# The 16 zb projection tiles: each 512-token matmul issued as two of 256 tokens, into two banks

## The chip, the cores and the metric

The kernel runs on one core of one Trainium2 chip. The time is device microseconds of one execution of the whole program. The kernel before took 2508.1 us (median of 3 runs, 2506.12 to 2508.59).

## The reference

One layer of a hybrid encoder trunk over 512 tokens of width 2048, all in float32. After an RMS norm `h` is multiplied by one wide weight matrix; its columns feed two branches, and one slice of it, `z_b` (2048 columns), is the gate of the convolution branch:

```python
h = rmsnorm(x, g_pre[i])
proj = h @ w_in[i]
qkv, z_a, b_raw, a_raw, glu_in, z_b, gate_logits = jnp.split(proj, ...)
...                                   # branch A: gated DeltaNet -> y_a
u = jax.nn.glu(glu_in, axis=-1)
u = causal_depthwise_conv(u, w_dw[i]) + b_dw[i]
u = jax.nn.silu(layernorm(u, ln_g[i], ln_b[i])) * jax.nn.silu(z_b)
y_b = u @ w_br_b[i]
gate_a, gate_b = jnp.split(jax.nn.sigmoid(gate_logits + b_gate[i]), 2, axis=-1)
mixed = (gate_a * y_a + gate_b * y_b) @ w_out[i]
x = x + rmsnorm(mixed, g_post[i])
...                                   # per-layer embedding -> output
```

## The kernel before

A projection is computed channel-major: one tile is 128 output channels (partitions of a PSUM bank) by all 512 tokens. Its inner dimension is 2048, in 16 slabs of 128. To keep float32 precision with the one-pass type fp32r, each operand is split into a high and a low part, and three products are summed: high weight by high `h`, high weight by low `h`, low weight by high `h` (lines 182, 184, 186 of `gemm_cm`). A tile is thus 16 x 3 = 48 matmuls, each with a 128x128 weight block as the stationary operand and 128x512 of `hT` as the moving one, all 48 summed into one bank. A weight block is loaded anew for each matmul: the page counts as many weight loads as matmuls (12202 each).

The weights arrive by DMA in pieces of 128x1024; `prep` cuts each in two, ScalarE rounds the high half (`CAST`, L127) and VectorE subtracts to get the low half (L128). The ring of split pieces holds four; one piece feeds 12 matmuls.

The order is written out by hand. Tiles are jobs in a list; after every matmul `tick()` is called, and it advances generators such as `layer_norm` every so many ticks, so their instructions fall between the matmuls. The 16 zb tiles (`evac_zb`, L828: SiLU from PSUM by ScalarE) stand after the tiles of branch A and before the gate-b and w_br_b tiles; while they run, `layer_norm` runs beside them: it sums means on TensorE (`mean_ps`, L779, and `rstd_ps`, L806, two passes of 128x512 fp32 each; `var_ps`, L794, four products of one column), works on VectorE, ScalarE and GpSimd, and at its end multiplies by each `zb[i]` (L817).

In this stretch two PSUM pools are open: `gps` (2 banks, tiles `g`) and `lps` (2 banks, the norm's). Two other loops are spoken of below: `gemm_tm` (L1212 to L1214), which walks over four banks and does three matmuls in each before it goes to the next, and the head scan's small fp32 products (`psB`, L468, 128x128).

Of the kernel before, what the change touches and what calls it, by code (L numbers as in the profile page):

```python
# [9 lines left out]
F32 = mybir.dt.float32  # L10
F32R = mybir.dt.float32r
AF = mybir.ActivationFunctionType
# [3 lines left out]
P = 128  # L16
T = 512
NTT = T // P
D = 2048
NK = D // P  # L20
# [12 lines left out]
ZB_TILE0 = 97  # L33
# [49 lines left out]
def _body(ctx, tc, A, out):  # L83
    nc = tc.nc
    PSUM = bass.MemoryType.PSUM
    mm = nc.tensor.matmul
# [27 lines left out]
    prep_src = deque()  # L114
    prepped = deque()

    def prep():
        if not prep_src:
            return
        src = prep_src.popleft()  # L120
        raw = rawp.tile([P, 1024], F32, tag="raw", name="raw", bufs=3)
        nc.sync.dma_start(raw, src)
        for q in range(2):
            rq = raw[:, q * T:(q + 1) * T]
            w = ring.tile([P, 1024], F32R, tag="w", name="w")
            hi, lo = w[:, 0:T], w[:, T:]
            nc.scalar.copy(hi, rq)  # L127
            nc.vector.tensor_tensor(lo, rq, hi.bitcast(F32), ALU.subtract)  # L128
            prepped.append((hi, lo))

    def next_piece():
        while len(prepped) < 3 and prep_src:
            prep()
        return prepped.popleft()

    jobs = deque()
# [5 lines left out]
    def tick():  # L142
        for a in list(active):
            a[2] -= 1
            if a[2] <= 0:
                steps = next(a[0], "end")
                if steps == "end":
                    active.remove(a)
                else:
                    a[2] = steps or a[1]  # L150
# [7 lines left out]
    def run_jobs():  # L158
        while jobs:
            jobs.popleft()()  # L160
# [3 lines left out]
    gps = gps_ctx.enter_context(tc.tile_pool(name="gps", bufs=2, space=PSUM))  # L164

    def w_in_tile(t):
        return A["w_in"][t]

    def gemm_cm(src, rhs, evac):
        if src is not None:  # L170
            prep_src.extend([src[0], src[1]])

        def job():
            ps = gps.tile([P, T], F32, tag="g", name="g")
            for qt in range(4):
                hi, lo = next_piece()
                for kk in range(4):
                    k = qt * 4 + kk
                    rh, rl = rhs[k]
                    wh = hi[:, kk * P:(kk + 1) * P]  # L180
                    wl = lo[:, kk * P:(kk + 1) * P]
                    mm(ps, wh, rh, start=(k == 0), stop=False)  # L182
                    tick()
                    mm(ps, wh, rl, start=False, stop=False)  # L184
                    tick()
                    mm(ps, wl, rh, start=False, stop=(k == NK - 1))  # L186
                    tick()
            evac(ps)
        jobs.append(job)

    hT = []
# [544 lines left out]
    def low(n, name, dt=F32R):  # L736
        return lop.tile([P, T], dt, tag="lop", name=name) if n < LOP else s2.tile([P, T], dt, tag="s2", name=name)
# [87 lines left out]
    def evac_zb(i):  # L825
        def f(ps):
            z = low(0, "zb", F32)
            nc.scalar.activation(z, ps, AF.Silu)  # L828
            zb[i] = z
        return f  # L830

    jobs.append(lambda: spawn(layer_norm(), 10))
    for i in range(NK):
        gemm_cm(w_in_tile(ZB_TILE0 + i), hT, evac_zb(i))
    mixT = [None] * NK

    def evac_yb(i):
# [79 lines left out]
        gemm_cm(A["w_br_b"][i], uT, evac_yb(i))  # L917
    lnp_ctx = ExitStack()
    lnp = lnp_ctx.enter_context(tc.tile_pool(name="lnp", bufs=1))
    lps = lnp_ctx.enter_context(tc.tile_pool(name="lps", bufs=2, space=PSUM))  # L920
    run_jobs()
    lnp_ctx.close()
# [140 lines left out]
    def run(products, side=None):  # L1063
        ps = {}
        for q in range(4):
            for pr in products:
                piece = next_piece_sw()
                if q == 0:
                    ps[pr] = [bank() for _ in range(2)]
                for t in range(2):  # L1070
                    mms(ps[pr][t], pr, piece, q, t)
                if side:
                    side()
        return ps
# [68 lines left out]
    def stepper(gen, n=1):  # L1143
        def f(k=None):
            for _ in range(n):
                next(gen, None)
        return f
# [9 lines left out]
    ps = run(("P1", "Q5"), stepper(gen))  # L1157
# [6 lines left out]
    ps = run(("P6", "P7", "P3"), stepper(gen))  # L1164
# [7 lines left out]
    ps = run(("P2", "Q4"))  # L1172
# [5 lines left out]
    ps = run(("P1", "Q5"))  # L1178
# [5 lines left out]
    ps = run(("P6", "P3"))  # L1184
# [4 lines left out]
    ps = run(("P2",))  # L1189
# [3 lines left out]
    ps = run(("P7",), stepper(pgen))  # L1193
# [5 lines left out]
    ps = run(("Q4",), stepper(pgen, 3))  # L1199
# [84 lines left out]
    for tt in range(NTT):  # L1284
        ps = fps.tile([P, T], F32, tag="f", name="f")
        for k in range(NK):
            wh, wl = held[k]
# [71 lines left out]
```

## Time and profile before

| | |
|---|---|
| median of 3 runs | 2508.1 us (2506.12 to 2508.59) |
| the profiled execution | 2505.59 us, span 2503.8 us |
| TensorE matmul busy | 2472.1 us, 99% of the span, 12202 matmuls |
| TensorE weight load busy | 2037.6 us, 81%, 12202 loads |
| VectorE / ScalarE busy | 1655.5 us (66%) / 1053.2 us (42%) |
| granted TensorE clock | 0.999 of full over the span |

How to read it: matmuls are pipelined, so a row's duration (395 ns for 128x512) is longer than the distance from one start to the next. What a matmul costs the engine is that distance, and it is read from starts in the order of time. PE is the matmul, PEld the weight load, which is shown beside it. Times in rows are in us from the span's start, durations of one instruction in ns where a column says mean.

### The profile page before, as it was taken

Reading aid. Unit: us, or ns where it says so; the run is one execution under the profiler, and the core shown is the slowest. Engines: PE = TensorE matmul, PEld = TensorE weight load, DVE = VectorE, ACT = ScalarE, POOL = GpSimd, SP = SyncE. Lnnn points to the kernel's source line nnn. Section 1 sums busy time; section 2 is a strip of 40 time slices with the busy share of each in tenths; the row PEclk is TensorE's granted clock in tenths of the full one; section 3 lists DMA queues with packets and bytes.
Section 4 is the critical chain, followed back from the end, with each engine's and each line's share of the span. In section 5 each row is a group of like instructions: output and inputs, shape, how many; then the busy total and the mean of one; then the engine's idle time right before and its main releaser. Section 6 shows DMA issues by size and latency. Waiting matters only on the chain.

```text
span 2503.8 us, 32581 instructions
## 1 busy us (share of the span) xinstructions
PE 2472.1 (99%) x12202; PEld 2037.6 (81%) x12202; DVE 1655.5 (66%) x3092; ACT 1053.2 (42%) x2083; POOL 133.6 (5%) x151
## 2 busy tenths in 40 slices
PE   8999999999999999999999999999999999998998
PEld 7888888888888888888888888888888888786886
DVE  6776767767677766886877879947323334877644
ACT  6555555555645555322222222235322223544532
POOL 0100000100000000000000000011000000100000
PEclk9999999999999999999999999999999999999999
DMA  7322222222122222323232323422222222776542
GB/s 260 118 94 71 93 72 85 81 81 91 66 92 81 77 85 76 110 97 109 97 109 97 107 99 110 169 85 102 99 100 94 97 97 100 189 229 196 202 169 76
DMA packets 85406, 279.45 MB, mean 112 GB/s; under 512 B 9472, under 2 KB 9728, under 8 KB 85248
## 3 DMA queue, kind: packets, MB, share of 16 engines
q1 hardware_dynamic: 81792, 266.89, 30.8%
q0 software_dynamic: 2304, 8.39, 1.8%
q10 hardware_dynamic: 1152, 2.10, 0.3%
q8 instruction: 95, 1.56, 0.2%
q14 instruction: 63, 0.52, 0.1%
HBM read 262.66 MB, written 14.68 MB: 111 GB/s over the span
## 4 chain that ended last, share of the span: by engine, by line
PE 93%; DVE 3%; DMA 2%; issue 1%; ACT 0%; POOL 0%; SPq 0%; DVEq 0%; POOLq 0%; ACTq 0%
PE g L184 26%; PE g L186 25%; PE g L182 25%; PE f L1213 2%; PE f L1214 2%; PE f L1212 2%; DMA raw<-in_w_out 2%; PE psB L468 1%; PE psS L474 1%; PE psA L462 1%; PE f L1057 1%; PE f L1058 1%; PE f L1056 1%; DVE wsp L1033 1%; PE pg L569 1%
## 5 line engine op out<-in xcount | busy, mean ns | idle before, releaser
L186 PE MATMUL g<-hh,w 128*128 128x512 f32 x2320 | 915.8, 395 | 1.6 <-DVE w L128 1.6
L184 PE MATMUL g<-hl,w 128*128 128x512 f32 x2320 | 916.3, 395 | 0.0
L182 PE MATMUL g<-hh,w 128*128 128x512 f32 x2320 | 913.5, 394 | 0.0
L128 DVE TENSOR_TENSOR w<-raw,w 128x512 fp32r<-128x512 f32 x780 | 552.8, 713 | 446.5 <-ACT w L127 444.5
L127 ACT CAST w<-raw 128x512 fp32r<-128x512 f32 x780 | 478.0, 618 | 879.1 <-PE g L186 777.6
L186 PEld LDWEIGHTS g<-hh,w 128*128 128x128 f32 x2320 | 436.5, 188 | 88.9 <-DVE w L128 4.7
L184 PEld LDWEIGHTS g<-hl,w 128*128 128x128 f32 x2320 | 436.4, 188 | 86.3 <-issue 1.6
L182 PEld LDWEIGHTS g<-hh,w 128*128 128x128 f32 x2320 | 436.5, 188 | 84.2 <-issue 0.2
L689 DVE SCALAR_TENSOR_TENSOR uc<-sg,vec,uc 128x511 f32<-128x511 f32 (+14 forms) x480 | 351.6, 734 | 14.0 <-ACT uc L686 3.9
L410 DVE SCALAR_TENSOR_TENSOR cv<-g,vec,cv 128x511 f32<-128x511 f32 x144 | 106.4, 739 | 31.1 <-ACT cv L408 30.8
L186 PE MATMUL g<-oh,w 128*128 128x512 f32 x256 | 99.7, 389 | 0.0
L182 PE MATMUL g<-uh,w 128*128 128x512 f32 x256 | 99.7, 389 | 0.0
L182 PE MATMUL g<-oh,w 128*128 128x512 f32 x256 | 99.7, 389 | 0.0
L184 PE MATMUL g<-ul,w 128*128 128x512 f32 x256 | 99.7, 389 | 0.0
L186 PE MATMUL g<-uh,w 128*128 128x512 f32 x256 | 99.7, 389 | 0.0
L184 PE MATMUL g<-ol,w 128*128 128x512 f32 x256 | 99.7, 389 | 0.0
L604 DVE TENSOR_TENSOR prod<-UT,VT 128x2 f32<-128x2 f32 (+30 forms) x248 | 87.4, 353 | 6.6
L1057 PE MATMUL f<-wsp,oph 128*128 128x512 f32 x192 | 76.3, 398 | 5.9 <-DVE wsp L1033 5.9
L1056 PE MATMUL f<-wsp,oph 128*128 128x512 f32 x192 | 74.7, 397 | 2.8 <-ACT wsp L1032 2.7
L1213 PE MATMUL f<-w,xh 128*128 128x512 f32 x192 | 75.1, 391 | 2.0 <-DVE w L128 2.0
L1058 PE MATMUL f<-wsp,opl 128*128 128x512 f32 x192 | 75.2, 393 | 0.0
L1212 PE MATMUL f<-w,xh 128*128 128x512 f32 x192 | 75.2, 392 | 0.0
(298 smaller groups left out, 2661.3 us busy)
## 6 DMA issues: line engine op xcount, KB each, us to landing
raw<-in_w_in SPq DMA_DIRECT2D x290, 512.0 KB, 3.2
raw<-in_w_ple_gate SPq DMA_DIRECT2D x40, 512.0 KB, 3.9
raw<-in_w_out SPq DMA_DIRECT2D x35, 512.0 KB, 4.9
raw<-in_w_br_a SPq DMA_DIRECT2D x32, 512.0 KB, 3.3
raw<-in_w_br_b SPq DMA_DIRECT2D x32, 512.0 KB, 3.2
t<-in_w_out POOLq DMA_DIRECT2D x16, 512.0 KB, 8.1
rw<-in_w_out SPq DMA_DIRECT2D x9, 512.0 KB, 4.6
x<-in_x SPq DMA_DIRECT2D x8, 512.0 KB, 9.4
```

The lines of the kernel that those rows point to most:

```text
L127: nc.scalar.copy(hi, rq)
L128: nc.vector.tensor_tensor(lo, rq, hi.bitcast(F32), ALU.subtract)
L182: mm(ps, wh, rh, start=(k == 0), stop=False)
L184: mm(ps, wh, rl, start=False, stop=False)
L186: mm(ps, wl, rh, start=False, stop=(k == NK - 1))
L410: nc.vector.scalar_tensor_tensor(y[:, s:], ps[:, 0:T - s], vv(w0 + 3 - s), y[:, s:], ALU.mult, ALU.add)
L689: nc.vector.scalar_tensor_tensor(y[:, s:], u[:, 0:T - s], vv(w0 + TAPS - 1 - s), y[:, s:], ALU.mult, ALU.add)
L1056: mm(ps, lh, wh[:, c], start=kk == 0, stop=False)
L1057: mm(ps, lh, wl[:, c], start=False, stop=False)
L1058: mm(ps, ll, wh[:, c], start=False, stop=kk == 7)
L1212: mm(ps[tt], lh, wh, start=k == 0, stop=False)
L1213: mm(ps[tt], lh, wl, start=False, stop=False)
```

## The change

`gemm_halves` replaces `gemm_cm` for the 16 zb tiles alone. For each of the 48 products it issues two matmuls with the same weight block: tokens 0 to 255 into the first half of a `gps` bank, tokens 256 to 511 into the first half of a bank of a new pool `nps` (2 banks). `tick()` is called after each pair, so a tile still has 48 ticks. The SiLU is done in two halves, one from each bank.

```diff
+    def gemm_halves(src, rhs, evac):
+        prep_src.extend([src[0], src[1]])
+
+        def job():
+            ps = [gps.tile([P, T], F32, tag="g", name="g"), nps.tile([P, T], F32, tag="n", name="n")]
+            for qt in range(4):
+                hi, lo = next_piece()
+                for kk in range(4):
+                    k = qt * 4 + kk
+                    rh, rl = rhs[k]
+                    wh = hi[:, kk * P:(kk + 1) * P]
+                    wl = lo[:, kk * P:(kk + 1) * P]
+                    for m, (w, r) in enumerate(((wh, rh), (wh, rl), (wl, rh))):
+                        for n in range(2):
+                            mm(ps[n][:, 0:256], w, r[:, n * 256:n * 256 + 256],
+                               start=k == 0 and m == 0, stop=k == NK - 1 and m == 2)
+                        tick()
+            evac(ps)
+        jobs.append(job)
...
             z = low(0, "zb", F32)
-            nc.scalar.activation(z, ps, AF.Silu)
+            for n in range(2):
+                nc.scalar.activation(z[:, n * 256:n * 256 + 256], ps[n][:, 0:256], AF.Silu)
             zb[i] = z
...
     for i in range(NK):
-        gemm_cm(w_in_tile(ZB_TILE0 + i), hT, evac_zb(i))
+        gemm_halves(w_in_tile(ZB_TILE0 + i), hT, evac_zb(i))
...
     lnp = lnp_ctx.enter_context(tc.tile_pool(name="lnp", bufs=1))
+    nps = lnp_ctx.enter_context(tc.tile_pool(name="nps", bufs=2, space=PSUM))
     lps = lnp_ctx.enter_context(tc.tile_pool(name="lps", bufs=2, space=PSUM))
```

On TensorE, at the first zb tile (the two rows ahead are the end of a w_br_a tile; `hh` and `hl` are high and low `hT`, `w` the split weights, `g` and `n` the banks), there stood before:

```order
6780 L184 MATMUL g<-ol,w 128x512
6781 L186 MATMUL g<-oh,w 128x512
6782 L182 MATMUL g<-hh,w 128x512
6783 L184 MATMUL g<-hl,w 128x512
6784 L186 MATMUL g<-hh,w 128x512
6785 L182 MATMUL g<-hh,w 128x512
```

and there stands now:

```order
6780 L184 MATMUL g<-ol,w 128x512
6781 L186 MATMUL g<-oh,w 128x512
6782 L205 MATMUL g<-hh,w 128x256
6783 L205 MATMUL n<-hh,w 128x256
6784 L205 MATMUL g<-hl,w 128x256
6785 L205 MATMUL n<-hl,w 128x256
6786 L205 MATMUL g<-hh,w 128x256
6787 L205 MATMUL n<-hh,w 128x256
```

Each row of 512 tokens has become two rows of 256 on alternating banks; the products stand in the same order, and the norm's own matmuls stand between the same products as before.

On ScalarE, at the sixth zb tile, where the norm's squares (`lsq`) share the engine with the weight casts and the SiLU, there stood before:

```order
803 L127 CAST w<-raw 128x512
804 L828 ACTIVATE zb<-g 128x512
805 L127 CAST w<-raw 128x512
806 L787 ACTIVATE lsq<-ur 128x512 x4
807 L127 CAST w<-raw 128x512
```

and there stands now:

```order
808 L127 CAST w<-raw 128x512
809 L849 ACTIVATE zb<-g 128x256
810 L849 ACTIVATE zb<-n 128x256
811 L127 CAST w<-raw 128x512
812 L807 ACTIVATE lsq<-ur 128x512 x4
813 L127 CAST w<-raw 128x512
```

The SiLU is two rows, at the same place between the casts; nothing else has moved here.

## Rows read from the trace of the kernel before

**Rows 1.** The page: span, busiest engine, the chain that ended last.
```profile
span 2503.8 us, 32581 instructions
...
PE 2472.1 (99%) x12202; PEld 2037.6 (81%) x12202; DVE 1655.5 (66%) x3092; ACT 1053.2 (42%) x2083; POOL 133.6 (5%) x151
...
PE 93%; DVE 3%; DMA 2%; issue 1%; ACT 0%; POOL 0%; SPq 0%; DVEq 0%; POOLq 0%; ACTq 0%
```

**Rows 2.** Busy time by engine over the zb tiles; last: clock, DMA share, GB/s.
```profile
1613.70:1793.20 179.50, 177.93 (x784) 146.15 (x783) 99.31 (x145) 76.79 (x130) 22.52 (x14) 1.00 0.31 109
```

**Rows 3.** Order of time, TensorE matmuls, in a zb tile: start, duration, instruction.
```profile
1639.90 0.39 PE L182 MATMUL g<-hh,w 128*128 128x512 f32 x1
1640.12 0.39 PE L184 MATMUL g<-hl,w 128*128 128x512 f32 x1
1640.35 0.39 PE L186 MATMUL g<-hh,w 128*128 128x512 f32 x1
```

**Rows 4.** The same stretch, weight loads.
```profile
1639.90 0.19 PEld L184 LDWEIGHTS g<-hl,w 128*128 128x128 f32 x1
1640.13 0.19 PEld L186 LDWEIGHTS g<-hh,w 128*128 128x128 f32 x1
```

**Rows 5.** Order of time, ScalarE, over one zb tile.
```profile
1624.46 0.60 ACT L828 ACTIVATE zb<-g 128x512 f32<-128x512 f32 x1 [0.80 <-PE g L186]
1624.95 0.61 ACT L127 CAST w<-raw 128x512 fp32r<-128x512 f32 x1
1627.18 0.62 ACT L127 CAST w<-raw 128x512 fp32r<-128x512 f32 x1 [1.61 <-PE g L186]
...
1635.34 0.60 ACT L828 ACTIVATE zb<-g 128x512 f32<-128x512 f32 x1 [2.10 <-PE g L186]
```

**Rows 6.** Order of time around the norm's mean (two fp32 passes of 512 columns), and the weight load behind.
```profile
1672.31 1.02 PE L779 MATMUL mean_ps<-acc,cst 128*128 128x512 f32 x2
1672.74 0.19 PEld L186 LDWEIGHTS g<-hh,w 128*128 128x128 f32 x1 [0.24 <-issue]
```

**Rows 7.** Weight loads behind the last of the norm's one-column products.
```profile
1714.71 0.19 PEld L184 LDWEIGHTS g<-hl,w 128*128 128x128 f32 x1
1714.82 0.19 PEld L186 LDWEIGHTS g<-hh,w 128*128 128x128 f32 x1
```

**Rows 8.** Four fp32 passes of 128 columns in a head scan, and what follows.
```profile
188.76 0.60 PE L468 MATMUL psB<-Xz,VP 128*128 128x128 f32 x4
...
189.09 0.19 PEld L182 LDWEIGHTS g<-hh,w 128*128 128x128 f32 x1
```

**Rows 9.** Matmuls of gemm_tm, which goes to another bank at each L1212.
```profile
2440.27 0.39 PE L1214 MATMUL f<-w,xl 128*128 128x512 f32 x1
2440.50 0.39 PE L1212 MATMUL f<-w,xh 128*128 128x512 f32 x1
2440.72 0.39 PE L1213 MATMUL f<-w,xh 128*128 128x512 f32 x1
```

**Rows 10.** Matmuls just behind a pause of TensorE in the zb tiles.
```profile
1688.66 0.50 PE L186 MATMUL g<-hh,w 128*128 128x512 f32 x1 [0.33 <-DVE w L128]
1689.00 0.40 PE L182 MATMUL g<-hh,w 128*128 128x512 f32 x1
1689.23 0.40 PE L184 MATMUL g<-hl,w 128*128 128x512 f32 x1
1689.47 0.40 PE L186 MATMUL g<-hh,w 128*128 128x512 f32 x1
```

**Rows 11.** Waits of TensorE over the zb tiles.
```profile
PE g L186 <- DVE w L128: 1.6, 2, 1.2
```

**Rows 12.** VectorE ahead of the second of these waits.
```profile
1691.59 0.69 DVE L789 TENSOR_TENSOR acc<-acc,lsq 128x512 f32<-128x512 f32 x1 [1.18 <-POOL acc L789]
1692.20 0.68 DVE L128 TENSOR_TENSOR w<-raw,w 128x512 fp32r<-128x512 f32 x1
```

**Rows 13.** A ScalarE evacuation of 128 columns, head scan.
```profile
189.49 0.36 ACT L471 ACTIVATE vz<-psB,c_all 64x128 f32<-64x128 f32 x1
```

## The prediction

> **What bounds the kernel now.** I read the page first: TensorE is busy 99% of the span, and the chain that ended last is 93% TensorE [rows 1]. So nearly every ns that a matmul takes more or less shows in the time, unless TensorE waits at that place. Next the table by stretch for the zb tiles: TensorE is busy 177.93 of 179.50 us at full granted clock (1.00, the 2.4 GHz level), VectorE 99.31, ScalarE 76.79, DMA share 0.31 [rows 2]. The other engines have room; the matmul stream is the bound.
>
> Then the order of time inside a tile. Matmuls start 0.22 to 0.23 us apart [rows 3]. The exact distance comes from two evacuations of successive tiles in an undisturbed part: 1624.46 and 1635.34, 10.88 us for 48 matmuls, 226.7 ns each [rows 5]. The weight load of the next matmul starts within 0.01 us of the start of the matmul ahead of it, and lasts 0.19 us [rows 3, 4]: it is hidden, one matmul ahead.
>
> **What a 512-column matmul consists of.** The norm's mean is two fp32 passes of 512 columns. The first starts at 1672.31; the load behind the second, which by the same pattern starts with it, stands at 1672.74 [rows 6]. So a pass is 0.43 us, at 2.4 GHz 1032 cycles, two a column and next to nothing over. Half of that, one cycle a column, is 213.3 ns, 13.3 ns short of the 226.7 that an fp32r matmul takes. This leftover is what the change turns on: is it paid per matmul, or per column?
>
> **The change, part by part.**
>
> *The matmuls.* 16 tiles x 48 = 768 matmuls of 512 columns go, 1536 of 256 come, each with its own weight load. No column is added; the norm's products keep their places. The streams are 2 x 106.7 = 213.3 ns, as before. With the leftover paid per matmul a pair is 2 x (106.7 + 13.3) = 240 ns, 13.3 more than now: 768 x 13.3 ns = +10.2 us. With it paid per column a pair is 226.7: 0. The trace has no 256-column fp32r matmul, so both sides are bounded by the nearest rows. Below: no matmul follows another faster than weight loads of 128 columns follow each other, and those are 0.11 us apart [rows 7]; four fp32 passes of 128 columns, which at two cycles a column stream exactly as long as 256 in fp32r, also start (189.09 - 188.76) / 3 = 0.11 us apart, load and stream side by side [rows 8]. A pair at 0.22 gives 768 x (-6.7 ns) = -5.1 us. Above: just behind a pause of TensorE the same 512-column matmuls stand (1689.47 - 1689.00) / 2 = 0.235 us apart, a leftover of 21.7 ns [rows 10]. If this is what a load and a stream cost each other when they don't fall into step, and halves never do, a pair is 2 x 128.4 = 256.7 ns: +23.0 us.
>
> I take +10.2. The reason is rows 10 against rows 3: the leftover grows from 13 to 22 ns with the same columns, so it is no rate of columns but something that happens between one matmul and the next. The fp32 passes have the same stationary blocks and show no such leftover, which leaves open what it is.
>
> *The second bank.* A new bank at each matmul could save a wait on the bank, or cost one. Neither: in gemm_tm the step into another bank (L1214 to L1212) is 0.23 us, the step within one (L1212 to L1213) 0.22 [rows 9]. Value 0, inside the bounds above.
>
> *The evacuation.* One SiLU of 512 columns (0.60 us) becomes two of 256. The nearest row on the other side, 128 columns, is 0.36 us [rows 13]; two halves are 0.72 to 1.2, so 0.12 to 0.6 us more on ScalarE a tile. Behind it in ScalarE's queue stand the weight casts, for which VectorE and then TensorE wait. In a quiet tile the next cast but one waits 1.61 us for TensorE to give a ring slot back [rows 5]; that idle time hides the extra. In the four or so tiles in which the norm's squares fill ScalarE the cover can be gone; there 4 x 0.6 = 2.4 us is the most it can cost. In all the zb tiles TensorE waits for VectorE alone [rows 11], so the value is 0.
>
> *The waits that a slower TensorE no longer meets.* TensorE waits twice, 1.6 us together, for low halves of weights [rows 11]. VectorE is late there because the norm's accumulation stands ahead of the subtraction, and waits itself for GpSimd (1.18 us) [rows 12]: a chain that starts at the mean and doesn't depend on the matmul rate. From 1672.31 to the second wait, some 19 us, a TensorE that is 13.3 / 226.7 = 5.9% slower comes 1.1 us later, and that much of the waiting goes. Late next is the matmul stream itself. Value -1.1 us (bounds -1.6 and 0).
>
> **Sum.** +10.2 + 0 + 0 - 1.1 = +9.1 us. The profiled execution took 2505.59 us, so it would take 2514.7; it lies 2.5 below the median of the runs shown, and on that median the forecast is 2508.1 + 9.1 = 2517.2, said as 2517.
>
> **The rivals.**
>
> *Per column, no change (2507 to 2509).* The leftover is a rate (one part in sixteen of the stream) and follows the columns; the load of 0.11 us just fits under a 113 ns stream. For it: the 226.7 ns is steady over whole tiles. Against it: rows 10. The pair stays at 226.7, the time at 2508.
>
> *The weight load decides, faster (2503).* If the leftover belongs to long fp32r streams or to the return to the same bank, halves on alternating banks drop it, and the next limit is the load, 0.11 us. This rival ends on the other side: it decides as soon as stream plus leftover falls under 113.3 ns a half. A pair is 0.22 us, -5.1 us. For it: rows 8, where load and stream of this length run at 0.11. Against it: the streams of rows 8 are fp32, which had no leftover at any length, and rows 9, where a change of bank takes nothing off.
>
> On TensorE: Matmul & The Clock Gate in the Trainium skill ("Back-to-back issue gap" and "LDWEIGHTS (loading the stationary operand)") gives a gap of columns over 2.4 plus 2.5 ns, and a load of columns over 1.2: 109 ns a half and 107 a load, by which this rival's pair would be about 218 ns. The trace differs from it at 512 columns, where the same rule gives 216 and the rows 226.7.
>
> *Load and stream collide (2520 to 2531).* The leftover is that of rows 10 throughout, because with halves a load runs beside the stream all the time and never has the free half of a matmul that it has now: +23.0 us, less the 1.6 of the two waits, about 2529.
>
> *The load is not hidden under a half (2670).* If a load had to follow the stream, a half would be 0.107 + 0.11 = 0.217 us and a pair 0.434: 768 x 207 ns = +159 us. Rows 3 and 4 speak against it: load and stream of the same full blocks already lie side by side.
>
> The same page of the Trainium skill ("The mechanism", under packing small matmuls) says that a load overlaps a matmul in flight only where the two use different row groups, by which all of these would be in series. The trace does not agree: 226.7 ns is 213.3 of stream and 13.3 over, with 0.19 us of load inside it.
>
> **How the numbers follow.** Chances: per matmul (the forecast) 0.50; per column 0.20; load decides 0.13; collide 0.14; not hidden 0.03. The forecast's own range, with the leftover between 10 and 16 ns, is 2513 to 2521. For eight in ten I reach down through the per-column case and into half of the load's (2505), and up into the collision (2529). About 0.2%, 5 us, is what a measurement of this kernel can tell from no change. Slower by more: nearly all of the forecast (0.47), the two costly rivals (0.17) and the upper edge of the per-column case (0.03), 0.67. Within: 0.03 of the forecast, 0.15 of per column, 0.07 of the load's, 0.25. Faster: 0.08.
>
> **What the profile after would show.** Right: successive halves 0.12 us apart, tiles 11.5 us apart (48 x 240 ns) instead of 10.88, 1536 matmuls of 128x256 with 1536 loads in the zb tiles, the stretch of 179.5 us some 9 us longer, and TensorE's waits there below 1.6 us. Halves 0.113 apart, with tiles still at 10.88: per column. Tiles at 10.6 with loads 0.11 apart: the load decides. Halves 0.13 apart or unsteady: collision. The evacuation step is wrong if TensorE now waits for casts (L127); the one on waits is wrong if the two waits stay at 1.6 us although the tiles have become longer. Any difference outside the zb tiles would make the whole account wrong, since every other matmul stands in the same order as before.

## The result, and the profile after

The changed kernel takes 2514.82 us (median of 5 runs, 2510.93 to 2516.3) against 2507.71 before (5 runs): a ratio of 1.0031, 95% interval 1.0020 to 1.0042, which is 5.0 to 10.5 us. It is slower, as forecast: the medians lie 7.1 us apart, the +9.1 us of the sum lie inside the interval, and the forecast of 2517 is 2 us over the median.

The page after, the lines that answer to [rows 1]:

```profile
span 2513.9 us, 34132 instructions
...
PE 2483.6 (99%) x12970; PEld 2079.7 (83%) x12970; DVE 1655.0 (66%) x3092; ACT 1054.2 (42%) x2099; POOL 133.9 (5%) x151
...
PE 94%; DVE 2%; DMA 2%; issue 1%; ACT 0%; POOL 0%; SPq 0%; DVEq 0%; POOLq 0%; ACTq 0%
```

768 matmuls and 768 weight loads more (12970 against 12202), and nearly the same share of TensorE in the chain (94%, was 93%). Busy time by engine over the zb tiles, from the same start to some 0.6 us behind the start of the last SiLU, as there, answers to [rows 2] (columns as there):

```profile
1613.70:1802.10 188.40, 187.49 (x1550) 186.23 (x1550) 100.40 (x145) 77.75 (x146) 22.25 (x14) 1.00 0.31 104
```

What changed is the weight load's column: 186.23 of 188.40 us busy, where it was 146.15 of 179.50. There is nearly always a load under way now. In the order of time, matmuls and loads of a zb tile, which answer to [rows 3, 4]:

```profile
1640.04 0.28 PE L205 MATMUL g<-hh,w 128*128 128x256 f32 x1
1640.04 0.19 PEld L205 LDWEIGHTS n<-hh,w 128*128 128x128 f32 x1
1640.16 0.28 PE L205 MATMUL n<-hh,w 128*128 128x256 f32 x1
```

Halves start 0.12 us apart. The first halves' SiLU of successive tiles in ScalarE's order of time, answering to [rows 5]:

```profile
1636.52 0.38 ACT L849 ACTIVATE zb<-g 128x256 f32<-128x256 f32 x1 [2.14 <-PE g L205]
1636.80 0.38 ACT L849 ACTIVATE zb<-n 128x256 f32<-128x256 f32 x1
...
1648.04 0.38 ACT L849 ACTIVATE zb<-g 128x256 f32<-128x256 f32 x1 [2.14 <-PE g L205]
```

A tile is 11.52 us, or 96 x 120.0 ns, where it was 10.88. The waits of TensorE over the zb tiles, answering to [rows 11]:

```profile
PE g L205 <- DVE w L128: 0.9, 1, 0.9
```

One wait of 0.9 us is left of two with 1.6. From the first SiLU to the first of the last tile it was 1624.46 to 1792.60, 168.14 us, and is 1625.00 to 1801.55, 176.55: +8.4 for 15 tiles, where 15 x 0.64 = 9.6 would be due; 1.2 us are given back. With the first tile, the stretch is +9.0 us. The profiled execution's span is 10.1 us longer; the other 1.1 us lie behind the zb tiles (711.2 us before, 712.3 after), in instructions that stand in the same order. The same stretch took 710.1 us in e2's profile and 711.9 in e1's, so a us or two there tells of one execution, not of the change.

### The profile page after: what moved, and what is told of

It is laid out like the page before. It is cut to its first block, busy times and chain, and to the rows that moved or that the text cites. A ratio compares the mean times of both kernels' runs of the same rounds, so it can differ in the third digit from the quotient of the medians.

```text
span 2513.9 us, 34132 instructions
## 1 busy us (share of the span) xinstructions
PE 2483.6 (99%) x12970; PEld 2079.7 (83%) x12970; DVE 1655.0 (66%) x3092; ACT 1054.2 (42%) x2099; POOL 133.9 (5%) x151
## 4 chain that ended last, share of the span: by engine, by line
PE 94%; DVE 2%; DMA 2%; issue 1%; ACT 0%; POOL 0%; SPq 0%; DVEq 0%; POOLq 0%; ACTq 0%
PE g L184 23%; PE g L186 23%; PE g L182 23%; PE g L205 3%; PE n L205 3%; DMA raw<-in_w_out 2%; PE f L1235 2%; PE f L1236 2%; PE f L1234 2%; PE psB L488 1%; PE psS L494 1%; PE f L1079 1%; PE f L1080 1%; PE f L1078 1%; PE psA L482 1%
## 5 line engine op out<-in xcount | busy, mean ns | idle before, releaser
L184 PE MATMUL g<-hl,w 128*128 128x512 f32 x2064 | 816.4, 396 | 0.0
L186 PE MATMUL g<-hh,w 128*128 128x512 f32 x2064 | 815.7, 395 | 0.0
L182 PE MATMUL g<-hh,w 128*128 128x512 f32 x2064 | 814.0, 394 | 0.0
L184 PEld LDWEIGHTS g<-hl,w 128*128 128x128 f32 x2064 | 388.3, 188 | 76.2 <-issue 1.4
L205 PE MATMUL g<-hh,w 128*128 128x256 f32 x512 | 134.5, 284 | 0.9 <-DVE w L128 0.9
L205 PE MATMUL n<-hh,w 128*128 128x256 f32 x512 | 134.1, 284 | 0.0
L205 PEld LDWEIGHTS n<-hh,w 128*128 128x128 f32 x512 | 98.4, 192 | 0.3 <-issue 0.2
L1079 PE MATMUL f<-wsp,oph 128*128 128x512 f32 x192 | 76.9, 402 | 4.5 <-DVE wsp L1055 4.5
```

What stands on the lines that cost most here:

```text
L205: mm(ps[n][:, 0:256], w, r[:, n * 256:n * 256 + 256], start=k == 0 and m == 0, stop=k == NK - 1 and m == 2)
L1079: mm(ps, lh, wl[:, c], start=False, stop=False)
```

## The experiments

The forecast rested on 13.3 ns over the columns, paid per matmul (theory A). The first five runs take it apart; the later ones ask what it is made of. Tile distances are read from the SiLU's starts, 48 or 96 matmuls apart. What is "over" is what a step takes beyond one cycle a column at the full clock: beyond 106.7 ns for 256 columns and 213.3 for 512. The diffs are shortened (`...` stands for code left out) and set against the changed kernel, that of e2 against the kernel before.

**One bank (e1).** Both halves in one bank, one SiLU:

```diff
-            ps = [gps.tile([P, T], F32, tag="g", name="g"), nps.tile([P, T], F32, tag="n", name="n")]
+            ps = gps.tile([P, T], F32, tag="g", name="g")
...
+                            c = slice(n * 256, n * 256 + 256)
-                            mm(ps[n][:, 0:256], w, r[:, n * 256:n * 256 + 256],
+                            mm(ps[:, c], w, r[:, c], ...)
```

> Halves of 256 tokens as in the changed kernel, but both into one bank and one SiLU of 512 columns. Theory A (13.3 ns per fp32r matmul beside its columns, whatever the bank): halves 120 ns apart, tiles 11.52 us, some 7 to 9 us slower than before, the same as the changed kernel. Rival B (alternating banks are what costs): halves at 113 ns, time as before. Rival B' (alternating banks spared something): more than 120 ns, more than 9 us slower.

Measured: 2513.23 us against 2504.76, ratio 1.0039 (1.0027 to 1.0052). The SiLU in ScalarE's order of time:

```profile
1637.89 0.60 ACT L849 ACTIVATE zb<-g 128x512 f32<-128x512 f32 x1 [2.26 <-PE g L206]
1649.41 0.60 ACT L849 ACTIVATE zb<-g 128x512 f32<-128x512 f32 x1 [2.26 <-PE g L206]
```

11.52 us again: the second bank neither costs nor spares anything. Rivals B and B' fall.

**The evacuation alone (e2).** The kernel before, with the SiLU in two halves:

```diff
-            nc.scalar.activation(z, ps, AF.Silu)
+            for n in range(2):
+                c = slice(n * 256, n * 256 + 256)
+                nc.scalar.activation(z[:, c], ps[:, c], AF.Silu)
```

> The kernel before with nothing but the SiLU of the zb tiles in two halves of 256 columns. Theory A: two SiLU of 0.38 us instead of one of 0.60, hidden, no change of time (within 2 us), TensorE's waits in the zb tiles stay near 1.6 us. Rival E (the evacuation carries a part of the cost): up to 16 x 0.16 = 2.6 us slower, with waits of TensorE for casts.

Measured: 2506.13 us against 2504.76, ratio 1.0004 (0.9995 to 1.0013). TensorE's waits over the zb tiles and just behind:

```profile
PE g L186 <- DVE w L128: 1.6, 2, 1.3
```

No wait for a cast, the same waits for VectorE: hidden. The time alone, -1.3 to +3.3 us, would leave room for the 2.6 us of rival E; the waits don't.

**The gate-b tiles too (e3).** Another 16 tiles in halves, where the norm is done:

```diff
-        gemm_cm(w_in_tile(GATE_TILE0 + 16 + i), hT, evac_gate(gate_b, i, 16 + i))
+        gemm_halves(w_in_tile(GATE_TILE0 + 16 + i), hT, evac_gate_halves(i))
```

> The changed kernel with the 16 gate-b tiles done in halves as well (another 768 matmuls split, in a stretch where TensorE waits for nothing). Theory A: another 768 x 13.3 ns = 10.2 us, none of it given back by waits, so 17 to 19 us slower than before, halves at 120 ns in both stretches. Rival F (the cost is special to the norm's stretch, by contention with its VectorE and ScalarE work): under 4 us more than the changed kernel.

Measured: 2525.12 us against 2504.76, ratio 1.0081 (1.0067 to 1.0094), 16.8 to 23.5 us, around the 17 to 19 expected. The gate's sigmoids of two tiles in a row:

```profile
1814.08 0.47 ACT L931 ACTIVATE gt<-g,vec 128x256 f32<-128x256 f32 x1 [0.80 <-PE g L205]
...
1825.60 0.48 ACT L931 ACTIVATE gt<-g,vec 128x256 f32<-128x256 f32 x1 [2.14 <-PE g L205]
```

11.52 us here as well, with other work beside it. Rival F falls.

**Unequal cuts (e4, e5).** 384 and 128 tokens, then 320 and 192, the SiLU cut likewise:

```diff
-                        for n in range(2):
+                        for n, (c0, c1) in enumerate(((0, 384), (384, T))):
-                            mm(ps[n][:, 0:256], w, r[:, n * 256:n * 256 + 256],
+                            mm(ps[n][:, 0:c1 - c0], w, r[:, c0:c1],
```

> The changed kernel with each pair cut into 384 and 128 tokens. Theory A with a floor by the weight load (0.111 us): 384 takes 160 + 13.3 = 173.3 ns, 128 takes 111 ns, a pair 284 ns, 44 us slower than before. Rival D (120 ns is what a load takes beside an fp32r stream, no leftover plus stream): the short piece 120 ns, a pair 293 ns, 51 us. Without a floor by the load: 173.3 + 66.7 = 240 ns, 10 us.

> The changed kernel with each pair cut into 320 and 192 tokens. Theory A with a floor by the weight load: 133.3 + 13.3 = 146.7 ns and 111 ns (192 columns stream 80 + 13.3 = 93.3, under the floor), a pair 258 ns, 24 us slower than before. Rival D: short piece 120 ns, a pair 267 ns, 31 us. Without a floor: 240 ns, 10 us.

Measured: 2548.38 us against 2504.76, ratio 1.0173 (1.0157 to 1.0189) with 384 and 128; 2532.64 against 2506.21, ratio 1.0111 (1.0093 to 1.0130) with 320 and 192: 44 and 26 us, where theory A with its floor had 44 and 24. The steps between weight loads, with 384 and 128:

```profile
1640.02 0.19 PEld L205 LDWEIGHTS n<-hh,w 128*128 128x128 f32 x1
1640.20 0.19 PEld L205 LDWEIGHTS g<-hl,w 128*128 128x128 f32 x1
1640.31 0.19 PEld L205 LDWEIGHTS n<-hl,w 128*128 128x128 f32 x1
```

and with 320 and 192:

```profile
1640.29 0.19 PEld L205 LDWEIGHTS n<-hh,w 128*128 128x128 f32 x1
1640.44 0.19 PEld L205 LDWEIGHTS g<-hl,w 128*128 128x128 f32 x1
1640.55 0.19 PEld L205 LDWEIGHTS n<-hl,w 128*128 128x128 f32 x1
```

From the load that starts beside a short piece to the next it is 0.11 us both times, though 128 columns are 53 ns of stream and 192 are 80; in these tiles no two loads stand closer. The floor by the weight load is real, and rival D falls. But tiles of 13.76 and 12.42 us make pairs of 286.7 and 258.7 ns: less a short piece of 108.5 ns, 384 columns take 178 ns and 320 take 150, which is 18 and 17 ns over their columns, not 13.3.

This share-out goes by the loads. The matmuls' own starts draw the line inside the pair elsewhere, here with 384 and 128:

```profile
1639.91 0.22 PE L205 MATMUL n<-hh,w 128*128 128x128 f32 x1
1639.97 0.39 PE L205 MATMUL g<-hh,w 128*128 128x384 f32 x1
1640.20 0.22 PE L205 MATMUL n<-hh,w 128*128 128x128 f32 x1
```

The long piece starts 0.06 us behind the short one and is followed after 0.23. The load beside it starts at 1640.02, 0.05 us later than the matmul, where in the changed kernel the two start together. Counted so, the long piece bears nearly all of the pair's leftover. With either share-out the leftover is no constant 13.3 ns. TensorE waits 3.1 us in the zb tiles of e5, 1.1 of them once for a cast, and not at all in e4; the 1.5 us beyond the usual 1.6 account for most of what e5 takes over the 24 expected.

**Sixteen-bit reading (e6, e7).** Both operands read as bf16, the upper 16 bits of each word; whole and in halves:

```diff
-                    rh, rl = rhs[k]
+                    rh, rl = [x.bitcast(mybir.dt.bfloat16)[:, 1:2 * T:2] for x in rhs[k]]
+                    wh, wl = [x[:, ...].bitcast(mybir.dt.bfloat16)[:, 1:2 * P:2] for x in (hi, lo)]
```

> The zb tiles as before, whole matmuls of 512 tokens into one bank and one SiLU, but both operands read as bf16 (every second 16-bit word of the same tiles, the upper one), so the zb products lose their low bits. Theory G (the 13.3 ns belongs to fp32r): matmuls 213 to 217 ns apart, 768 x -10 to -13 ns = 8 to 10 us faster than before, less what the two waits for weights take back (up to 2 us). Rival H (it belongs to any matmul with its own weight load): 226.7 ns, no change.

> The same bf16 reading with the halves of the changed kernel. Theory G: halves 109 to 112 ns apart, at the weight load's spacing if that of bf16 is no shorter, a pair 218 to 224 ns, 2 to 7 us faster than before. Rival H: 120 ns, 9 us slower.

Measured: 2503.74 us, ratio 0.9994 (0.9985 to 1.0004), and 2505.89, ratio 0.9998 (0.9989 to 1.0008). Whole:

```profile
1636.14 0.60 ACT L845 ACTIVATE zb<-g 128x512 f32<-128x512 f32 x1 [2.08 <-PE g L203]
1646.94 0.60 ACT L845 ACTIVATE zb<-g 128x512 f32<-128x512 f32 x1 [2.08 <-PE g L203]
```

and halves:

```profile
1636.40 0.38 ACT L848 ACTIVATE zb<-g 128x256 f32<-128x256 f32 x1 [1.99 <-PE g L204]
...
1647.28 0.38 ACT L848 ACTIVATE zb<-g 128x256 f32<-128x256 f32 x1 [1.99 <-PE g L204]
```

10.80 us is 225.0 ns a matmul: 11.7 of the 13.3 ns over stay with another type, and theory G falls. 10.88 us is 113.3 ns a half, 6.7 over: rival H falls too. Read this way halves cost next to nothing (226.7 ns a pair), and the leftover goes with the columns. The type changes the weight load as well. In the halves its row lasts 97 ns, where it was 0.19 us in the changed kernel (rows from 1625 to 1670 us: count, busy us, mean ns, idle us before):

```profile
L204 PEld LDWEIGHTS <-w 128*128 128x128 bf16 x398 | 38.6, 97 | 6.5
```

**Fewer weight columns (e8, e9).** fp32r again, 64 weight columns a matmul:

```diff
-                    wh = hi[:, kk * P:(kk + 1) * P]
+                    wh = hi[:, kk * P:kk * P + 64]
...
-                            mm(ps[n][:, 0:256], w, r[:, n * 256:n * 256 + 256],
+                            mm(ps[n][0:64, 0:256], w, r[:, n * 256:n * 256 + 256],
```

> The kernel before, but each of the zb tiles' matmuls loads 64 weight columns instead of 128 and so computes 64 of the tile's 128 channels (the other 64 are filled with the same values). Theory J (what is over beyond the columns is paid for the weight load, in proportion to its columns): matmuls of 512 tokens 213.3 + 6.7 = 220 ns apart, tiles 10.56 us. Theory K (it is paid at the step from one matmul to the next, whatever is loaded): 226.7 ns, tiles 10.88 us.

> The changed kernel with 64 weight columns a matmul, so 64 of each tile's 128 channels. Theory J: halves 106.7 + 6.7 = 113.3 ns apart, tiles 10.88 us. Theory K: 120 ns, 11.52 us.

Measured, one run each: 2506.72 and 2507.55 us against 2504.66. Whole:

```profile
1636.68 1.19 ACT L847 ACTIVATE zb<-g 64x512 f32<-64x512 f32 x2 [2.14 <-PE g L204]
1647.72 1.19 ACT L847 ACTIVATE zb<-g 64x512 f32<-64x512 f32 x2 [2.14 <-PE g L204]
```

and halves:

```profile
1636.17 0.76 ACT L850 ACTIVATE zb<-g 64x256 f32<-64x256 f32 x2 [1.99 <-PE g L205]
...
1647.05 0.76 ACT L850 ACTIVATE zb<-g 64x256 f32<-64x256 f32 x2 [1.99 <-PE g L205]
```

Halves are 10.88 us, 113.3 ns each, as theory J had it: with half the weight columns, 6.7 of the 13.3 ns are gone. The load's row is shorter here too (the same stretch):

```profile
L205 PEld LDWEIGHTS g<-hh,w 128*64 128x64 f32 x134 | 18.0, 134 | 0.0
```

Each of the two runs without the 6.7 ns changes something else besides: e7 the type of the moving operand, e9 the number of outputs, 64 for 128. The shorter load is what they share. Whole matmuls miss both theories: 11.04 us, 230.0 ns, slower than with the full load. There the steps are unsteady; they go round through 224 to 236 ns. So theory J's number for halves came true and its rule, a price in proportion to the weight columns, did not.

**Sixteen bits side by side (e10, e11).** The same cut with fp16 words that lie next to each other:

```diff
+                    rh, rl = [x.bitcast(mybir.dt.float16)[:, 0:T] for x in rhs[k]]
+                    wh, wl = [x[:, ...].bitcast(mybir.dt.float16)[:, 0:P] for x in (hi, lo)]
```

> The zb tiles in whole matmuls with both operands read as fp16 words that lie side by side (the first 512 and 128 words of each block), so the zb values have nothing to do with the reference's; only the spacing is of interest. Theory L (what is over is the price of moving four bytes a column, which the strided bf16 reading also spans): 213 to 217 ns apart, tiles 10.2 to 10.4 us. Theory M (it isn't): 225 ns as with the strided reading, tiles 10.80 us.

> The same fp16 words in halves of 256 tokens. Theory L: 107 to 110 ns apart, tiles 10.3 to 10.6 us. Theory M: 113.3 ns as with the strided reading, tiles 10.88 us.

Measured, one run each: 2495.54 and 2502.2 us against 2504.66. Whole:

```profile
1633.97 0.60 ACT L845 ACTIVATE zb<-g 128x512 f32<-128x512 f32 x1 [1.97 <-PE g L203]
1644.33 0.60 ACT L845 ACTIVATE zb<-g 128x512 f32<-128x512 f32 x1 [1.97 <-PE g L203]
```

and halves:

```profile
1635.21 0.38 ACT L848 ACTIVATE zb<-g 128x256 f32<-128x256 f32 x1 [1.89 <-PE g L204]
...
1645.69 0.38 ACT L848 ACTIVATE zb<-g 128x256 f32<-128x256 f32 x1 [1.89 <-PE g L204]
```

215.8 and 109.2 ns, 2.5 ns over the columns both times: theory L. What was over with the strided reading is the price of a read that spans four bytes a column. TensorE: Matmul & The Clock Gate in the Trainium skill, under "Back-to-back issue gap", gives columns over 2.4 plus 2.5 ns for one matmul behind another. The trace agrees with it for these reads (215.8 and 109.2 ns), and not for fp32r (226.7 ns at 512 columns).

**Which of the two reads (e12).** Four ways by turns within one kernel:

```diff
+                    mv = slice(1, 2 * T, 2) if how % 2 == 0 else slice(0, T)
+                    st = slice(0, P) if how % 2 == 0 else slice(1, 2 * P, 2)
+                    rh, rl = [x.bitcast(mybir.dt.float16)[:, mv] for x in rhs[k]]
+                    wh, wl = [x[:, ...].bitcast(mybir.dt.float16)[:, st] for x in (hi, lo)]
```

> The zb tiles with both operands read as fp16 words, in four ways by turns (tile number modulo 4), so the zb values have nothing to do with the reference's: 0 halves with the moving words two apart and the weights side by side, 1 halves with the moving words side by side and the weights two apart, 2 as 0 in whole matmuls, 3 as 1 in whole matmuls. Theory N (the share that goes with the columns comes from the span of the moving read alone): 113 ns, 109 ns, 225 ns, 216 ns. Theory O (from the weight read): 109, 113, 216, 225. Theory Q (only both together): 109, 109, 216, 216.

Measured, one run: 2503.04 us against 2508.28. Ways 0 and 2, with the moving words two apart, in TensorE's order of time (ten steps of halves, then nine of whole matmuls):

```profile
1614.83 0.28 PE L210 MATMUL g<-hh,w 128*128 128x256 f16 x1
...
1615.96 0.27 PE L210 MATMUL g<-hl,w 128*128 128x256 f16 x1
...
1636.63 0.39 PE L208 MATMUL g<-hl,w 128*128 128x512 f16 x1
...
1638.67 0.39 PE L208 MATMUL g<-hl,w 128*128 128x512 f16 x1
```

(1615.96 - 1614.83) / 10 = 113 ns, and 2.04 / 9 = 227 ns. Ways 3 and 1, with the moving words side by side, in ScalarE's order:

```profile
1646.09 0.60 ACT L854 ACTIVATE zb<-g 128x512 f32<-128x512 f32 x1 [2.09 <-PE g L208]
1656.45 0.60 ACT L854 ACTIVATE zb<-g 128x512 f32<-128x512 f32 x1 [1.97 <-PE g L208]
...
1757.17 0.39 ACT L856 ACTIVATE zb<-g 128x256 f32<-128x256 f32 x1 [1.99 <-PE g L210]
...
1767.65 0.38 ACT L856 ACTIVATE zb<-g 128x256 f32<-128x256 f32 x1 [1.89 <-PE g L210]
```

10.36 / 48 = 215.8 ns and 10.48 / 96 = 109.2 ns, though their weights are two apart. Theory N: of the two reads it is the moving one alone.

## Why the prediction was right, and where its reason was not

*The time.* +9.1 us were forecast, 5.0 to 10.5 measured (7.1 between the medians); the profile's own stretch gained 9.0. Tiles at 11.52, halves at 0.12, TensorE's waits below 1.6 us are what it named for "right". It also named any difference outside the zb tiles as a sign against it; the 1.1 us behind them lie within what e1 and e2 show of one execution.

*The step on the matmuls, +10.2 us: the size holds, the reason half falls.* The prediction took the 13.3 ns as paid per matmul, since the leftover had grown behind a pause with the same columns [rows 10]: "it is no rate of columns but something that happens between one matmul and the next". That failed: a leftover that grows behind a pause shows a second part, and says nothing of the steady one. A rate of columns is all of a whole matmul's 13.3 ns and half of a half's: one part in sixteen of the stream, 6.7 ns a half, as the rival "per column" had it, shown by the 113.3 ns of halves with strided bf16 (e7), with 64 weight columns (e9) and with a wide moving read alone (e12), and by its absence with words side by side (e11). For fp32r itself, which can't be read side by side, the read is the cause by the equal figures. By that alone a pair would have stayed at 226.7 ns and the change would have cost nothing. What it costs is the other 6.7 ns of each half, and these go with the full fp32r weight load beside a short stream: they are there with a load of 0.19 us (120.0 ns a half) and gone with one of 134 or 97 ns (113.3, e9 and e7). That is the seed of the rival "collide": a load beside the stream all the time, at 6.7 ns over the columns' share instead of the 15 that I had set for it. 2 x (106.7 + 6.7 + 6.7) = 240 is the number that a constant 13.3 gives too. That the load's part came out as large as the part that the prediction had put in the wrong place is luck, as far as the runs show: the equal cut hid the difference, the unequal ones (17 and 18 ns over by the loads) showed it.

*The floor under "the load decides".* In the zb tiles no load of 128 weight columns followed another faster than 0.11 us, as the prediction had it (108.5 ns between loads, beside 128 and beside 192 columns). That no matmul follows another faster did not hold to the letter: the one behind 128 columns starts after 0.06 us, and the time is lost in the longer piece. This rival failed because the halves, at 120.0 ns, never came down to the floor.

*The load under a half.* Hidden, as rows 3 and 4 had said; the case at 2670 is out.

*The second bank, 0, and the evacuation, 0.* Both right: e1 has the same tiles with one bank, e2's interval ends 0.13% over the kernel before, and its waits are the same. The SiLU grew from 0.60 to 2 x 0.38 us, 0.16 a tile, near the lower bound of 0.12 to 0.6.

*The waits, -1.1 us.* 0.7 us less in the waits and 1.2 us less in the stretch. The rest of the 1.2 the prediction had not counted. By the starts, some 0.3 us is what a wait costs beyond its idle time, and there is one wait fewer: the first matmul behind a wait is followed after 0.34 us before [rows 10] and after 0.22 in the changed kernel. Some 0.2 us are slow steps: whole matmuls run at 224 to 236 ns for about ten steps behind each pause or fp32 product [rows 10], the halves at 114 to 120. In e3 TensorE waits for nothing in the stretch of the second 16 tiles, and nothing is given back.

*Open.* Why a full load adds 6.7 ns to a half of 256 columns and nothing steady to a whole matmul: that the load itself is slowed beside a wide read, or the stream by the load, the runs don't tell apart. No run shortens the load alone, with the moving operand left in fp32r and all 128 outputs. Nor do the runs explain the 230 ns of whole matmuls with 64 weight columns, or the 225.0 of strided bf16, where one part in sixteen gives 226.7. No version tried beats the kernel before clear of the noise: the side-by-side 16-bit reads are faster, but they compute something else.

## What to carry to other kernels

Read a matmul's cost from steps between starts over a whole tile, and compare it with columns at the granted clock; what is over may have several parts, and one size can't tell them apart, two sizes or an unequal cut can. Cutting an fp32r matmul of 512 columns in two doubles the weight loads. The cut cost 13.3 ns a pair at 256 columns, 32 with a piece of 192 and 60 with one of 128: there the loads of 128 weight columns stand at their closest, 0.11 us. A small steady loss per instruction on the engine that bounds is added up in full (768 x 13.3 ns), and the waits already there give a little back (1.2 us here, with what goes with a wait included).

## What the runs showed of the hardware

A moving operand whose columns lie four bytes apart streams about one part in sixteen slower than the granted clock gives (113.3 ns for 256 columns, 225 to 227 for 512), whatever the type read (fp32r, strided bf16 or fp16); 16-bit words side by side stream at the clock plus 2.5 ns (109.2 and 215.8). The same spacing of the stationary operand costs nothing (e12). fp32 passes, two cycles a column, show none of it [rows 6]. The row of a load of 128 weight columns lasts 0.19 us in fp32r and 97 ns in bf16 (e7). In the fp32r tiles cut unequally, loads stand no closer than 108 ns (e4, e5).
